# A two-layer hybrid block on one core: one shared pool of PSUM banks, new planner durations, two first projection blocks side by side, merged key-tile sums

## The chip, the core and the metric

The kernel runs on one core of a Trainium2 chip, as one program. The metric is the time of one execution on the device, in microseconds (us). The engines are TensorE (PE, matrix products; its weight loads are listed as PEld), VectorE (DVE), ScalarE (ACT), GpSimd (POOL) and SyncE (SP, which issues the DMAs here). TensorE writes to eight PSUM banks of 512 fp32 numbers per partition, and a matmul into a bank has to wait until what lay there before has been read.

## What is computed

Two layers over 528 positions (16 meta tokens and 512 inputs) with 1024 features, all in fp32. A layer is

```python
hn = rmsnorm(h, norm1_g[l])
sq, sk, sv, rq, rk, rv, rg, u = split(hn @ w_in[l])
sb_o = stick_breaking(rmsnorm(q), rmsnorm(k), v)      # 6 heads of 64
ro = retention(rotary(rmsnorm(q)), rotary(rmsnorm(k)), v)   # 6 heads of 64
ro = rmsnorm(ro) * silu(rg)
so = s5_mixer(u, ...)            # complex linear recurrence, 16 groups x 64 states
h = h + concat(sb_o, ro, so) @ w_out[l]
hn = rmsnorm(h, norm2_g[l])
h = h + (silu(hn @ w_gate[l]) * (hn @ w_up[l])) @ w_down[l]
```

In stick breaking a weight is exp(log_sigmoid(z) + between), where between is the sum of log_sigmoid(-z) over all later keys. The kernel gets these sums over keys as matmuls with matrices of ones.

## The kernel before

**Tiling.** Features lie on the 128 partitions, positions in the free dimension: a [128, 528] tile is one block of features, and a row of 528 takes two PSUM banks of 264 columns. Every large product is made of three fp32r products, of a high and a low part of the weights and of the activations (`mm3`, lines 347 to 356: for each block k of the contraction, wh*xh, wh*xl, wl*xh, each for two halves of the row). A weight block (`Unit`, line 273 on) is loaded by SP into one of two `wr` buffers, cast by ACT into its high part, and subtracted by DVE or POOL into its low part; four blocks are asked for ahead (`AHEAD`). A block of the input projection is 48 matmuls of 264 columns, and there are 23 of them in a layer.

**Side work.** Between two matmuls of a projection, `tick` (line 186) lets up to six waiting tasks go one step further. Tasks are Python generators: head norms, the lane of stick breaking (`sb_lane`, three pairs of heads one after the other), the lane of retention (`ret_lane`, three pairs) and the lane of the recurrence (`s5_lane`: `s5_mix` for two halves, then `s5_glu`). A task may go on when the time at which its last step should be done, by the planner, lies no later than `LEAD` after the planner's time on PE. The planner's durations stand in the three `Timed` wrappers (lines 125 to 127, a fixed part and a part for each element) and in `mm`. What is issued where follows from that; then a list scheduler orders each engine's queue, earlier-issued work first. On the chip each queue runs in that order. Nearly all instructions of DVE, ACT and POOL carry line 122 (the wrapper) and all matmuls line 134, so tiles are told apart by name.

**Banks.** The planner keeps count of banks: a task takes `banks(n)` out of `BANKS` = 2 (line 32) and gives them back after its result has been read; stick breaking takes its score banks out of a separate count `ZBANKS` = 4 (`take("scores", 2)`, line 872). Two of the eight banks are left for the projection that runs.

**The start.** `load_h(k)` (line 1037) loads the first weight block in four pieces right behind h[0] and ahead of h[1], and the second one whole behind h[4]. The first block's projection then runs alone, k by k, as `xh`, `xl` of h[k] come; the second and third follow. After the third (`HOLD` = 2) `nrm.finish` makes the norm's factors R. `first_params` is spawned ahead of all that: `s5_scalars` (line 452), a chain of some 95 small DVE instructions on [128, 16] tiles, and then `s5_params` (line 535), five tasks (`inputs` 0 and 1, `outputs`, `phasors` 0 and 1) on DVE and POOL, which `s5_lane` waits for (`par`). For the second layer `s5_params` runs during the first layer's MLP, on POOL alone.

**In `outputs`** (line 610), the imaginary half (`ri` = 1) is made on DVE by a `scalar_tensor_tensor` (-a - b) of two tiles `gx` that the engine of that half, POOL, has made.

**The sums of stick breaking** (`sb_group`, line 832). A group g is a list of key tiles (j, q0, q1, o0): key tile j, queries q0 to q1, at column o0 of a bank. `G_A` holds three key tiles for queries 0 to 272; `G_B2` three and `G_B1` two for queries 272 to 528. After two matmuls with the triangle `tri`, every key tile j of the group gets the sums of every later key tile i of the set: one pair of matmuls (high and low part) with `ones` for each pair (j, i). For `G_A` and `G_B2` these are 3 pairs with widths 144, 16 and 16; for `G_B1` they are 7, three of width 256, two of 144 and two of 16. Each set is made once for each of 6 heads in 2 layers.

## Time and profile before

| what | value |
|---|---|
| median of 3 runs (lowest to highest) | 1372.97 us (1372.7 to 1373.25) |
| profiled execution, its own time | 1372.14 us |
| span of that execution, first to last instruction | 1370.1 us |
| PE busy | 1335.6 us, 9188 matmuls |
| DVE, ACT, POOL busy | 791.4, 589.5, 464.9 us |
| mean granted TensorE clock | 0.994 |

The profiled execution is 0.83 us under the median, and 2.04 us of it lie outside the span. A row of a timeline gives the start and the length of an instruction, or of several in a row that are merged, their number (x), and in brackets how long the engine had been idle before it and what released it. A matmul's length includes its way through the array; what one more matmul costs in a row of them is the distance from start to start.

### The profile page before, as it was taken

Reading aid. Unit: us, or ns where it says so; the run is one execution under the profiler, and the core shown is the slowest. Engines: PE = TensorE matmul, PEld = TensorE weight load, DVE = VectorE, ACT = ScalarE, POOL = GpSimd, SP = SyncE. Lnnn points to the kernel's source line nnn. Section 1 sums busy time; section 2 is a strip of 40 time slices with the busy share of each in tenths; the row PEclk is TensorE's granted clock in tenths of the full one; section 3 lists DMA queues with packets and bytes.
Section 4 is the critical chain, followed back from the end, with each engine's and each line's share of the span. In section 5 each row is a group of like instructions: output and inputs, shape, how many; then the busy total and the mean of one; then the engine's idle time right before and its main releaser. Section 6 shows DMA issues by size and latency. Waiting matters only on the chain.

```text
span 1370.1 us, 22529 instructions
## 1 busy us (share of the span) xinstructions
PE 1335.6 (97%) x9188; PEld 1220.8 (89%) x9188; DVE 791.4 (58%) x1270; ACT 589.5 (43%) x936; POOL 464.9 (34%) x588
## 2 busy tenths in 40 slices
PE   6989999999899999999999999999999999999998
PEld 5988989989899999999999899998788888888886
DVE  8974657858456445533566874635485544554453
ACT  5447565446242223322355636664354422342231
POOL 5691545222799212200233451433222200220120
PEclk9999999999999999999999999999999999999999
DMA  4211222223221422232232221213232332333223
GB/s 157 70 62 47 84 66 87 78 69 98 95 79 48 123 78 93 93 93 93 78 93 93 71 94 47 92 43 102 62 123 93 92 95 90 99 102 93 92 81 104
DMA packets 38983, 118.26 MB, mean 86 GB/s; under 512 B 4960, under 2 KB 5472, under 8 KB 38880
## 3 DMA queue, kind: packets, MB, share of 16 engines
q1 hardware_dynamic: 38880, 116.82, 26.8%
q8 instruction: 72, 1.18, 0.4%
q14 instruction: 31, 0.25, 0.1%
HBM read 111.46 MB, written 2.10 MB: 83 GB/s over the span
## 4 chain that ended last, share of the span: by engine, by line
PE 82%; DVE 10%; POOL 3%; ACT 1%; issue 1%; DMA 1%; SPq 0%; DVEq 0%; ACTq 0%
PE pj L134 71%; PE z L134 5%; DVE ysm L122 2%; PE hps L134 1%; PE av L134 1%; PE ro L134 1%; DVE wl L122 1%; DVE s5w L122 1%; PE kps L134 1%; PE sc L134 1%; DVE gg L122 1%; DVE st L122 0%; DVE py L122 0%; POOL py L122 0%; DVE sp L122 0%
## 5 line engine op out<-in xcount | busy, mean ns | idle before, releaser
L134 PE MATMUL pj<-xh,wh 128*128 128x264 f32 (+1 forms) x1792 | 454.4, 311 | 16.8 <-ACT wh L122 5.1
L134 PE MATMUL pj<-xh,wl 128*128 128x264 f32 (+1 forms) x1792 | 453.3, 310 | 3.2 <-DVE wl L122 3.2
L134 PE MATMUL pj<-xl,wh 128*128 128x264 f32 (+1 forms) x1792 | 452.6, 310 | 2.6 <-DVE xl L122 2.6
L122 ACT CAST wh<-wr 128x1024 fp32r<-128x1024 f32 (+3 forms) x209 | 205.8, 987 | 418.8 <-PE pj L134 384.6
L134 PEld LDWEIGHTS pj<-xh,wh 128*128 128x128 f32 x1792 | 298.9, 190 | 36.0 <-issue 5.9
L134 PEld LDWEIGHTS pj<-xl,wh 128*128 128x128 f32 x1792 | 299.4, 190 | 20.5 <-DVE xl L122 3.3
L134 PEld LDWEIGHTS pj<-xh,wl 128*128 128x128 f32 x1792 | 298.9, 190 | 20.7 <-DVE wl L122 3.4
L122 DVE TENSOR_TENSOR wl<-wr,wh 128x1024 fp32r<-128x1024 f32 (+3 forms) x166 | 251.8, 1519 | 69.2 <-ACT wh L122 69.2
L134 PE MATMUL pj<-lo,wh 128*128 128x264 f32 (+1 forms) x720 | 193.4, 322 | 1.3 <-DVE lo L122 1.3
L134 PE MATMUL pj<-hi,wh 128*128 128x264 f32 (+1 forms) x720 | 193.2, 323 | 0.4 <-ACT hi L122 0.4
L134 PE MATMUL pj<-hi,wl 128*128 128x264 f32 (+1 forms) x720 | 193.1, 322 | 0.1
L122 POOL TENSOR_TENSOR up<-ga,up 128x528 f32<-128x528 f32 (+1 forms) x44 | 61.9, 1407 | 345.6 <-DVE up L122 345.5
L122 POOL TENSOR_TENSOR wl<-wr,wh 128x1024 fp32r<-128x1024 f32 (+2 forms) x43 | 96.2, 2237 | 159.4 <-ACT wh L122 153.6
L122 DVE TENSOR_TENSOR h<-h,pj 128x264 f32<-128x264 f32 (+1 forms) x144 | 69.1, 510 | 140.4 <-PE pj L134 140.0
L134 PEld LDWEIGHTS pj<-hi,wh 128*128 128x128 f32 x720 | 120.3, 189 | 11.9 <-ACT hi L122 0.7
L134 PEld LDWEIGHTS pj<-lo,wh 128*128 128x128 f32 x720 | 120.0, 188 | 12.1 <-DVE lo L122 1.5
L134 PEld LDWEIGHTS pj<-hi,wl 128*128 128x128 f32 x720 | 120.0, 189 | 11.1 <-DVE wl L122 0.5
L122 POOL TENSOR_TENSOR lo<-ga,hi 128x528 fp32r<-128x528 f32 (+1 forms) x44 | 58.5, 1330 | 158.0 <-ACT hi L122 157.9
L122 DVE TENSOR_TENSOR up<-pj,R 128x264 f32<-128x264 f32 (+1 forms) x66 | 32.1, 514 | 94.2 <-PE pj L134 94.2
L122 DVE TENSOR_TENSOR ga<-si,up 128x528 f32<-128x528 f32 (+1 forms) x44 | 31.7, 720 | 72.7 <-ACT si L122 57.2
L122 ACT ACTIVATE si<-si,bias 128x528 f32<-128x528 f32 (+1 forms) x44 | 32.2, 731 | 93.9 <-DVE si L122 93.9
L122 POOL TENSOR_TENSOR lo<-sp,hi 128x432 fp32r<-128x432 f32 (+2 forms) x36 | 44.4, 1245 | 73.3 <-ACT hi L122 71.7
(221 smaller groups left out, 1533.9 us busy)
## 6 DMA issues: line engine op xcount, KB each, us to landing
wr<-in_w_in_dram SPq DMA_DIRECT2D x45, 512.0 KB, 3.5
wr<-in_w_gate_dram SPq DMA_DIRECT2D x44, 512.0 KB, 3.5
wr<-in_w_up_dram SPq DMA_DIRECT2D x44, 512.0 KB, 3.5
wr<-in_w_down_dram SPq DMA_DIRECT2D x32, 512.0 KB, 3.6
wr<-in_w_out_dram SPq DMA_DIRECT2D x16, 384.0 KB, 3.3
wr<-in_w_down_dram SPq DMA_DIRECT2D x16, 384.0 KB, 3.1
rc<-in_rope_dram SPq DMA_DIRECT2D x12, 264.0 KB, 3.8
rs<-in_rope_dram SPq DMA_DIRECT2D x12, 264.0 KB, 4.0
```

Of the source, the lines that this page charges most:

```text
L122: return f(*a, **k)
L134: nc.tensor.matmul(out, lhsT=lhsT, rhs=rhs, start=start, stop=stop, skip_group_check=more)
```

## The change

Six edits: (1) all side work shares one count of six banks, of which stick breaking's scores may hold four at most; (2) the planner's durations are new, with a fixed part of 150 to 230 ns and other rates, by kind of instruction, and a double count for strided outputs; (3) the first two weight blocks are loaded and projected together, k by k (`two_proj`), with pieces of both between the h[k]; the squares of the norm are issued inside that loop, and `first_params` is spawned behind `nrm.finish`; (4) in `sb_group` the sums of one later key tile that go to two key tiles of the group are one matmul, whose moving operand is read twice and whose output has two pieces of the bank; (5) in `outputs` the half `ri` = 1 is an add on its own engine (POOL in both layers), with the sign moved into `bbd` and `xi`; (6) the task of `outputs` is planned 2 us later before the `kps` matmuls.

```diff
-BANKS = 2
+BANKS = 6
 ZBANKS = 4
...
-    V = Timed(nc.vector, "V", 70, 1.05)
-    SC = Timed(nc.scalar, "SC", 180, 0.7)
-    G = Timed(nc.gpsimd, "G", 110, 2.1)
+    V = Timed(nc.vector, "V", {"one": (150, 1.05), "two": (160, 1.2), "tensor_scalar": (150, 0.55),
+                               "tensor_tensor_scan": (180, 2.2)})
+    SC = Timed(nc.scalar, "SC", {"one": (230, 0.8), "two": (230, 0.8)})
+    G = Timed(nc.gpsimd, "G", {"one": (180, 2.1), "two": (180, 2.1), "memset": (100, 0.85)})
...
-                        if ri:
-                            V.scalar_tensor_tensor(out=o, in0=a, scalar=-1.0, in1=b, op0=ALU.mult, op1=ALU.subtract)
-                        else:
-                            sub(o, a, b)
+                        (add if ri else sub)(o, a, b)
...
-                    engines[ri].tensor_copy(
+                    engines[ri].tensor_scalar(
...
+            now[0][1] += 2000
...
-        behind = [(j, q0, q1, o0, i) for j, q0, q1, o0 in g for i in place if i > j]
...
+        behind = {}
+        for j, q0, q1, o0 in g:
+            for i, (g1, o1, p0) in place.items():
+                if i > j:
+                    a = max(q0, p0)
+                    behind.setdefault(i, (g1, o1 + a - p0, q1 - a, []))[3].append(o0 + a - q0)
...
+        for g1, o1, w, to in behind.values():
+            d, c = zp[:, to[0]:to[0] + w], slice(o1, o1 + w)
+            if len(to) == 2:
+                f = to[1] - to[0]
+                d = zp[:, to[0] + w - f:to[0] + w + f].rearrange("p (t c) -> p t c", t=2)[:, :, f - w:]
             for part in range(2):
-                mm(zp[:, o0 + a - q0:o0 + q1 - q0], lhsT=ones, rhs=hl[g1][part][:, o1 + a - p0:o1 + q1 - p0],
+                x = hl[g1][part][:, c]
+                mm(d, lhsT=ones, rhs=x[:, None, :].to_broadcast([P, 2, w]) if len(to) == 2 else x,
                    start=False, stop=True, more=True)
...
-        freed(1, "scores")
+        freed(1, "scores", "bank")
...
-                yield from take("scores", 2)
+                yield from take(2, "scores", "bank")
...
+    units += [Unit(*plan[0]), Unit(*plan[1])]
+    for k in range(KD):
         nc.sync.dma_start(out=h[k], in_=A["h0"][k])
...
+        q = []
+        if k < 4:
+            q = [(units[k % 2], k // 2, 4)]
+        elif k < 6:
+            q = [(units[k % 2], 1, 2)]
+        for u, i, pieces in q:
+            c = u.load(i, pieces)
+            nrm.parts(k)
+            for _ in u.split(c):
+                pass
+        if not q:
+            nrm.parts(k)
+        if k:
+            nrm.square(k - 1)
+    nrm.square(KD - 1)
...
-    spawn(first_params())
...
+        def two_proj():
+
+            ws = [weight(), weight()]
+            pss = [open_ps(T), open_ps(T)]
+            xh, xl = nrm.x
+            for k in range(KD):
+                for ps, w in zip(pss, ws):
+                    mm3(ps, tuple(t[:, k:k + 1, :] for t in w), (xh[k:k + 1], xl[k:k + 1]), first=k == 0, last=k == KD - 1)
+            return pss
...
             if i == HOLD[l]:
                 nrm.finish()
+                if l == 0:
+                    spawn(first_params())
```

## Rows read from the trace of the kernel before

**Rows 1.** The page, busy us (share of the span) xinstructions, PE.
```profile
PE 1335.6 (97%) x9188; PEld 1220.8 (89%) x9188; DVE 791.4 (58%) x1270; ACT 589.5 (43%) x936; POOL 464.9 (34%) x588
```
**Rows 2.** By stretch: length, busy PE PEld DVE ACT POOL, clock, DMA share, GB/s.
```profile
0.00:36.50 36.50, 23.50 (x148) 22.11 (x148) 30.51 (x97) 18.04 (x29) 21.85 (x45) 0.95 0.44 148
36.50:100.00 63.50, 58.15 (x437) 55.37 (x437) 53.49 (x139) 28.39 (x51) 50.52 (x117) 0.95 0.21 71
350.00:450.00 100.00, 94.75 (x764) 93.48 (x764) 54.52 (x68) 34.06 (x46) 94.35 (x208) 0.98 0.24 78
```
**Rows 3.** The same columns, in four us behind one of PE's longer waits.
```profile
30.00:34.00 4.00, 4.00 (x23) 4.00 (x22) 3.79 (x26) 1.32 (x2) 1.13 (x4) 0.57 0.64 255
```
**Rows 4.** Timeline of PE near 92 and 120 us: the sums of two groups.
```profile
92.17 0.23 PE L134 MATMUL z<-hi,ones 128*128 128x144 f32 x1
...
92.64 0.26 PE L134 MATMUL z<-lo,ones 128*128 128x16 f32 x1
92.75 0.49 PE L134 MATMUL pj<-xl,wh 128*128 128x264 f32 x2
...
119.73 0.39 PE L134 MATMUL z<-lo,tri 128*128 128x512 f32 x1
119.97 0.28 PE L134 MATMUL z<-hi,ones 128*128 128x256 f32 x1
...
120.21 0.23 PE L134 MATMUL z<-hi,ones 128*128 128x144 f32 x1
...
121.50 0.37 PE L134 MATMUL pj<-xh,wh 128*128 128x264 f32 x1
```
**Rows 5.** Timeline of PE in the first 36 us: start, length, idle before.
```profile
5.06 0.81 PE L134 MATMUL pj<-xh,wh 128*128 128x264 f32 x2 [5.06 <-ACT wh L122]
...
12.10 0.64 PE L134 MATMUL pj<-xh,wh 128*128 128x264 f32 x2
12.54 0.63 PE L134 MATMUL pj<-xl,wh 128*128 128x264 f32 x2
...
28.95 0.52 PE L134 MATMUL pj<-xh,wl 128*128 128x264 f32 x2 [3.19 <-DVE wl L122]
...
35.69 0.40 PE L134 MATMUL pj<-xh,wl 128*128 128x264 f32 x2
35.93 0.28 PE L134 MATMUL nps<-hi,meanw 128*128 128x264 f32 x1
```
**Rows 6.** Busy time by stretch of the instructions on tile s5w alone: DVE, ACT, POOL.
```profile
0.00:36.50 36.50, 18.70 (x65) 0.41 (x2) 0.00 (x0) 0.95 0.44 148
```
**Rows 7.** Timeline of DVE and POOL at 12.8 us: two instructions beside each other.
```profile
12.80 2.41 POOL L122 TENSOR_TENSOR wl<-wr,wh 128x1024 fp32r<-128x1024 f32 x1 [1.90 <-ACT wh L122]
12.93 2.38 DVE L122 TENSOR_SCALAR s5w<-s5w 128x16 f32<-128x16 f32 x2
```
**Rows 8.** Timeline of PE and DVE between 77 and 86 us.
```profile
77.44 0.39 PE L134 MATMUL pj<-xh,wh 128*128 128x264 f32 x1 [2.52 <-ACT we L122]
85.16 0.76 DVE L122 TENSOR_TENSOR u<-pj,R 128x264 f32<-128x264 f32 x2
```
**Rows 9.** Timeline of PE, DVE and POOL during the first layer's MLP.
```profile
371.61 0.56 PE L134 MATMUL pj<-xh,wh 128*128 128x264 f32 x1 [3.78 <-DVE ga L122]
368.07 2.94 DVE L122 SCALAR_TENSOR_TENSOR gg<-gx,gx 64x320 f32<-64x320 f32 x4 [3.96 <-POOL gx L122]
359.01 3.47 POOL L122 TENSOR_TENSOR gg<-gx,gx 64x320 f32<-64x320 f32 x4
413.51 0.41 PE L134 MATMUL kps<-gg,bbd 128*32 128x128 f32 x2 [1.47 <-POOL bbd L122]
```
**Rows 10.** Timeline of DVE and PE: the recurrence's lane in the first layer.
```profile
114.80 5.11 DVE L122 COPY uc<-u 32x132 f32<-32x132 f32 x8
155.17 1.06 PE L134 MATMUL es<-uc,we 128*128 128x132 f32 x8
281.96 0.51 PE L134 MATMUL pj<-lo,wh 128*128 128x264 f32 x2 [1.26 <-DVE lo L122]
```

More of the change, by code (lines that the diff above doesn't have):

```diff
@@ L107, in hybrid_kernel, with __init__ @@
     class Timed:
-        def __init__(self, eng, key, fixed, each):
-            self.eng, self.key, self.fixed, self.each = eng, key, fixed, each
+        def __init__(self, eng, key, kinds):
+            self.eng, self.key, self.kinds = eng, key, kinds
         def __getattr__(self, name):
@@ L117, in issue @@
                 o = k.get("out", a[0] if a else None)
-                n = 1
-                for d in o.shape[1:]:
-                    n *= d
-                spend(self.key, self.fixed + self.each * n)
+                n = math.prod(o.shape[1:]) * (2 if o.ap[-1][0] > 1 else 1)
+                two = [x for x in (k.get("in0"), k.get("in1")) if x is not None]
+                kind = name if name in self.kinds else "two" if len(two) == 2 and not any(
+                    x.space == PSUM for x in two) else "one"
+                fixed, each = self.kinds[kind]
+                spend(self.key, fixed + each * n)
                 return f(*a, **k)
             return issue
-    V = Timed(nc.vector, "V", 70, 1.05)
-    SC = Timed(nc.scalar, "SC", 180, 0.7)
-    G = Timed(nc.gpsimd, "G", 110, 2.1)
+    V = Timed(nc.vector, "V", {"one": (150, 1.05), "two": (160, 1.2), "tensor_scalar": (150, 0.55),
+                               "tensor_tensor_scan": (180, 2.2)})
+    SC = Timed(nc.scalar, "SC", {"one": (230, 0.8), "two": (230, 0.8)})
+    G = Timed(nc.gpsimd, "G", {"one": (180, 2.1), "two": (180, 2.1), "memset": (100, 0.85)})
     def mm(out, lhsT, rhs, start, stop, more=False):
-        n = out.shape[-1] / 2.4
-        t = 2 * max(107.0, 2 * n) if rhs.dtype == F32 else max(107.0, n) + 3
+        n = math.prod(out.shape[1:]) / 2.4
+        t = 2 * max(109.0, 2 * n + 3) if rhs.dtype == F32 else max(110.0, 1.055 * n + 5)
         spend("PE", t / 2 if 64 in (rhs.shape[0], out.shape[0]) else t)
@@ L172, in hybrid_kernel, with take, freed @@
     free = {"bank": BANKS, "scores": ZBANKS, "group": GROUPS}
-    def take(what, n):
-        if free[what] < n:
-            yield lambda: free[what] >= n
-        free[what] -= n
+    def take(n, *what):
+        if any(free[w] < n for w in what):
+            yield lambda: all(free[w] >= n for w in what)
+        for w in what:
+            free[w] -= n
     def banks(n):
-        yield from take("bank", n)
-    def freed(n, what="bank"):
-        free[what] += n
+        yield from take(n, "bank")
+    def freed(n, *what):
+        for w in what or ("bank",):
+            free[w] += n
     def tick(most=TICKS):
@@ L881, in sb_pair @@
         sets = ((G_A,), (G_B2, G_B1))
-        yield from take("group", 2)
+        yield from take(2, "group")
         started.append(weights(sets[0]))
@@ L887, in sb_pair @@
             if groups is sets[0]:
-                yield from take("group", 4)
+                yield from take(4, "group")
                 started.append(weights(sets[1]))
@@ L1034, in ret_pair @@
         res.append(o)
-    def load_h(k):
+    nrm = Norm(0, 48)
+    units += [Unit(*plan[0]), Unit(*plan[1])]
+    for k in range(KD):
         nc.sync.dma_start(out=h[k], in_=A["h0"][k])
@@ L1040, in load_h @@
             nc.sync.dma_start(out=cols, in_=A["cols"])
-            u = Unit(*plan[0])
-            u.parts = ()
-            for i in range(4):
-                for _ in u.split(u.load(i, 4)):
-                    pass
-            units.append(u)
-        elif k == 4:
-            u = Unit(*plan[1])
-            u.load()
-            u.parts = u.split()
-            units.append(u)
-            u.use()
-            splits[0] = 2
-    nrm = Norm(0, 48)
-    for k in range(KD):
-        load_h(k)
-        nrm.parts(k)
+        q = []
[13 more added lines that the diff above has]
+    nrm.square(KD - 1)
+    for u in units:
+        u.parts = ()
+    splits[0] = 2
     for i in (90, 96):
         G.tensor_scalar(out=cols[:, i:i + 2], in0=cols[:, i:i + 2], scalar1=0.125, scalar2=None, op0=ALU.mult)
-    for k in range(KD):
-        nrm.square(k)
     par = []
@@ L1075, in hybrid_kernel, with proj @@
         mix = [None] * 8
-        def proj(n, p):
-            w = weight()
+        def proj(w):
             ps = open_ps(T)
@@ L1129, in hybrid_kernel @@
         for i, (n, p) in enumerate(proj_order(l)):
-            held.append((n, p, proj(n, p)))
+            if l == 0 and i < 2:
+                if i == 0:
+                    first = two_proj()
+                held.append((n, p, first[i]))
+            else:
+                held.append((n, p, proj(weight())))
             if i == HOLD[l]:
                 nrm.finish()
+                if l == 0:
+                    spawn(first_params())
             if i >= HOLD[l]:
```

13 lines of the change are left out of this document (5 added, 8 removed).

## The prediction, made before the changed kernel was run

> **What bounds the kernel now.** I read the page first, then the busy time by stretch, then PE's timeline where it sits idle, then DVE and POOL at the same places. PE is busy 1335.6 of 1370.1 us [rows 1]: the reader is to see that only two things can be gained, PE's own work and its 34.5 us of idle time. The idle time is bunched: 36.50 - 23.50 = 13.0 us in the first 36.5, 63.50 - 58.15 = 5.35 us from there to 100, and 5.25 us between 350 and 450 [rows 2]; 10.9 us are scattered over the rest. A wait costs more than its length: after a wait of 3.19 us [rows 5] the granted clock was 0.57 over four us, the lower of its two levels (1.2 instead of 2.4 GHz) for 3.4 us of them, which is (1 - 0.57) x 4 = 1.7 us more [rows 3]. For the stretches, (1 - 0.95) x 63.5 = 3.2 us and (1 - 0.98) x 100 = 2.0 us [rows 2].
>
> **A, the merged sums.** Fewer matmuls in a stretch that PE bounds. A group of the kind of G_A or G_B2 issues six, from 92.17 to 92.75, 0.58 us; one of width 16 costs 0.11 [rows 4]. After it there are four: the pair of width 144, which stays, and one pair of width 32 for two pairs of width 16, at 0.11 each as before, so 0.22 less; as two neighbours of different width can share some of it, I take 0.19. G_B1 issues fourteen, 119.97 to 121.50, 1.53 us. After it eight: a pair of 256 at 0.24 (119.97 to 120.21), a pair of 512 at 2 x 0.24 (119.73 to 119.97), a pair of 288 at 0.27 (between those two), a pair of 32 at 0.22; 1.21 us, 0.32 less [rows 4]. 24 groups x 0.19 + 12 x 0.32 = 8.4 us, on the path, for 120 matmuls less. No row shows a moving operand that is read twice or an output in two pieces. From below: if a merged one costs as much as its two parts, 0. Worse: if each costs twice its width, 24 x 0.03 + 12 x 0.65 = 8 us are lost. I take -8.4, since width alone set the distance in every row here; ends +8 and -9.5.
>
> **B, the start.** A block is 48 matmuls at 0.12 (35.69 to 35.93 for two), three are 17.3 us; the third ends at 35.93 and the first matmul starts at 5.06 [rows 5], so 13.6 us are lost between them. One block alone offers six matmuls for each h[k], and h[1] stands in SP's queue behind four weight pieces; two blocks offer twelve, and h[1] stands behind one. SP issues 15 DMAs instead of 14, with the same bytes, so the last h[k] comes about when it did. Now the start: 5.06 (the first piece of weights still has to come) + 17.3 + the slow clock + a rest. At 12.10 two matmuls still take 0.44 instead of 0.24 [rows 5]; if the slow spacing again lasts to 13 us, 8 us hold 36 matmuls instead of 66, 3.6 us lost. DVE's s5w chain, 18.70 us busy in this stretch [rows 6], is out of it, so the wait for wl at 28.95, 3.19 us [rows 5], should go. The norm's squares move up in ACT's queue, between the high parts; ACT is busy 18.0 of 36.5 us [rows 2], so the cast of the third block behind them finds room. For the waits that stay (xl at DVE's pace, unit 1's low part behind POOL's constants) I put 2.5. Sum 28.5 us instead of 35.9: -7.4. Ends: no rest and a shorter slow stretch, -10; the third block's low part as late as now, with its clock, -2.5.
>
> **C, 36 to 100 us.** Waits and clock cost 5.35 + 3.2 = 8.5 us here [rows 2]. At 77.44 PE waits for a bank; the evacuation of block u, done before by DVE's queue order, comes at 85.16, behind a run of phasor instructions [rows 8]. The larger planned durations space those tasks, so evacuations fall between them. Against it: the s5w chain now comes behind the third block. DVE's 53.5 us [rows 2] + 18.7 [rows 6] - 2.9 (the subtractions that go to POOL, by the same work in [rows 9]) = 69.3 us, in the 71.5 us from 28.5 to 100. The three evacuations issued ahead of the chain free six banks, so PE has three blocks (17 us) before it misses the next evacuation; behind the chain wait the head norms' products and the low part of every third weight block. That is nearly full, so I take half the gain, -4; ends -8.5 and +8 (the second rival).
>
> A row speaks against moving the subtractions to POOL: a POOL subtraction ran from 12.80 for 2.41 us, and two DVE instructions of 16 columns beside it took 2.38 us together and ended with it [rows 7]. The Trainium skill (SBUF — State Buffer, section "SBUF: two separate sides") has it that the two engines share a pair of ports as an exclusive lock, held for the whole instruction, so that the loser stands still; the trace agrees. By that rule the four adds, 3.47 / 4 = 0.87 us each [rows 9], could stop DVE for up to 3.5 us in this stretch, C would be -0.5 and the time 3.5 us longer.
>
> **D, the MLP of the first layer.** PE waits 3.78 us at 371.61 for DVE to read ga; DVE had stood idle for 3.96 us at the head of its queue with the four subtractions gg, which wait for POOL's gx, and then worked on them for 2.94 us, with ga behind them [rows 9]. The change takes these four off DVE. Next late there: POOL's product up, on which DVE's later ga waits. POOL is busy 94.35 of 100 us [rows 2] and gets four more instructions, some 3.5 us [rows 9]. The wait of 1.47 us for bbd [rows 9] is what the 2 us of edit 6 are put against. The two are all 5.25 us of idle, with the clock 7.25 us; I take -6. Ends -7.25 and -2 (a POOL that is late by 3.5 us puts PE into a new wait).
>
> **E, the rest.** The shared banks remove no PE work. 10.9 us of idle are scattered outside B, C and D; some of it, as the last transfer of the output, nothing here touches, and 1.26 us are the wait for the recurrence's result at 281.96 [rows 10]. Two banks for all of head norms, retention and recurrence hold lanes back: uc is done at 114.80 + 5.11 = 119.9 and its first product es comes at 155.17, 35 us later [rows 10]. With six that should shrink. But stick breaking, which had four banks for itself, now competes; and PE comes about 20 us sooner to the output projection that needs the lanes. I take 0, ends -4 and +10. The signs moved in bbd and xi are the same instructions on the same engines: 0, bounded by tenths.
>
> **The sum.** -8.4 - 7.4 - 4 - 6 + 0 = -25.8 against the profiled execution's 1372.14 us: 1346.3. The median of the runs is 0.83 us above that execution: 1347.2.
>
> **Rivals.** (1) All waits in reach go: -9.5 - 10 - 8.5 - 7.25 - 4 = -39, 1334. For it: each has a cause that an edit names. Against: orders made anew make waits of their own. (2) DVE becomes the bound between 28 and 100: its idle time there is dependency and can't be used, so 18.7 - 2.9 = 15.8 us more work lengthen the stretch by 15.8 less the 7.4 of the earlier start: C is +8, 1359. For it: the 69.3 of 71.5 us. Against: part of the 18.70 are instructions held up by POOL [rows 7]. (3) The merged matmuls don't pay: A is 0 to +8, 1356 to 1364. (4) Slower: the recurrence is late. Its scalars now start behind nrm.finish, at some 30 us instead of 5, and the load of braw goes behind more weight loads in SP's queue with them; if the chain to uc keeps its length, uc starts at 114.8 + 25 = 140, and with a lane as long as now (114.8 to 281.96, 167 us [rows 10]) its result comes at 307. PE would be there at 281.96 - 7.4 - 4 - half of A = 266. It would wait up to 41 us, 1347 + 41 = 1388. It decides from 29 us on; below that the gain is larger than the wait. Against it: the 35 us between uc and es are a wait for banks that the change widens, and most of those 41 us are in them. (5) No change within what can be told: the new order gives back what the rest brings.
>
> **How the numbers follow.** Forecast, near 1347: 0.62. Rival 1: 0.08; rival 2: 0.12; rival 3: 0.07; rival 4: 0.08; rival 5: 0.03. The range for 8 in 10 runs from rival 1's 1334 to rival 3's 1364: it holds the forecast's, rival 2's and rival 3's 0.81, and leaves half of rival 1 below and 4 and 5 above. Faster by over 0.2% (2.7 us, about what a measurement of this kernel can tell from no change): 0.62 + 0.08 + 0.12 + 0.07 = 0.89; within it 0.03; slower 0.08.
>
> **What would show it.** A: 120 matmuls less, the sums of a G_B1 group within 1.2 us. B: nps at 27 to 30 us, no wait for wl ahead of it. C: no PE wait over one us and no half-clock stretch between 36 and 100; if rival 2 holds, waits for DVE's evacuations or wl there. D: no wait near 370 for ga, gg's four adds on POOL. E: es within some us of uc; PE waiting for lo of the recurrence at the output projection would be rival 4. Wrong would be the forecast, in its sum even if not in its parts, if PE's idle time stayed above 25 us.

## The result: slower by 1.2 per cent

| what | before | after |
|---|---|---|
| median (lowest to highest) of 4 runs each, same chip | 1373.1 us (1372.7 to 1373.25) | 1388.48 us (1387.08 to 1391.19) |
| ratio, 95% interval | | 1.0117 (1.0105 to 1.0129) |
| span of the profiled execution | 1370.1 us | 1389.5 us |
| mean granted clock | 0.994 | 0.978 |

The forecast was 1347; the time lies above its whole range, at the time of the fourth rival. The profiled execution of the changed kernel took 1391.19 us, 2.7 above its median.

First the page's line of busy times, of the changed kernel; it answers to [rows 1].

```profile
PE 1340.9 (97%) x9068; PEld 1222.3 (88%) x9068; DVE 784.7 (56%) x1261; ACT 588.1 (42%) x937; POOL 470.9 (34%) x598
```

The 120 matmuls are gone, and PE is nevertheless busy for 5.3 us longer and idle for 48.5 us instead of 34.5. Where, the busy time by stretch tells (length, busy PE, PEld, DVE, ACT, POOL, clock, DMA share, GB/s). The first two stretches are those of [rows 2]; then the rest of the in-projection; from the first matmul of the output projection's part (0,1,2) to the first of part (6,7); and six blocks of the first MLP, from the start of its fifth to the start of its eleventh. First the changed kernel:

```profile
0.00:36.50 36.50, 28.17 (x196) 27.32 (x196) 31.18 (x95) 19.61 (x33) 21.57 (x47) 0.95 0.49 162
36.50:100.00 63.50, 57.65 (x414) 53.55 (x413) 50.87 (x134) 33.10 (x62) 47.27 (x104) 0.92 0.19 63
100.00:253.30 153.30, 145.50 (x1096) 133.30 (x1094) 91.65 (x167) 78.49 (x153) 67.74 (x63) 0.96 0.23 73
253.30:304.40 51.10, 41.19 (x311) 37.89 (x309) 37.46 (x76) 20.93 (x41) 12.53 (x12) 0.85 0.12 37
360.20:409.70 49.50, 40.24 (x306) 39.63 (x305) 19.43 (x24) 15.90 (x23) 43.58 (x70) 0.86 0.21 70
```

The last three stretches of the same work in the kernel before:

```profile
100.00:252.40 152.40, 151.51 (x1204) 139.64 (x1202) 94.55 (x184) 85.28 (x164) 62.63 (x48) 1.00 0.23 73
252.40:280.20 27.80, 27.05 (x230) 25.52 (x226) 21.72 (x44) 18.22 (x33) 10.54 (x10) 1.00 0.21 58
344.40:386.10 41.70, 37.92 (x302) 37.74 (x301) 21.05 (x25) 13.49 (x18) 35.41 (x39) 0.96 0.24 83
```

The reader is to see the row of 253.3 to 304.4. Both kernels begin the output projection at the same moment, 252.4 and 253.3 us. The changed one then needs 51.1 us instead of 27.8: PE idles for 9.9 us of them (0.75 before), its clock is 0.85 (1.00 before), and it works off 311 matmuls instead of 230. 144 of either number are part (0,1,2); the rest, 167 and 86, is side work that the planner had left for this place (a row counts every matmul that overlaps its stretch; by their starts it is 165 and 81, as in the table below).

PE's timeline there, in the changed kernel, shows its waits: for retention's third pair (`kt`, `sc`, `hsq`) and for the recurrence's result (`hi`), which [rows 10] shows before. Below them stand two rows of ACT.

```profile
284.79 2.08 PE L138 MATMUL kv<-rv,kt 128*128 128x128 f32 x8 [5.26 <-ACT kt L125]
...
287.28 3.09 PE L138 MATMUL sc<-rm,rm 64*128 64x128 f32 x16 [0.25 <-DVE sc L125]
...
298.33 1.16 PE L138 MATMUL hps<-hsq,blk 128*128 128x264 f32 x4 [0.86 <-ACT hsq L125]
...
304.41 2.13 PE L138 MATMUL pj<-hi,wh 128*128 128x264 f32 x8 [3.46 <-ACT hi L125]
306.33 0.65 PE L138 MATMUL pj<-lo,wh 128*128 128x264 f32 x2
```
```profile
283.62 0.64 ACT L125 ACTIVATE y<-ysm 128x528 f32<-128x528 f32 x1 [3.80 <-DVE ysm L125]
284.17 0.57 ACT L125 COPY kt<-rtp 128x512 f32<-128x512 f32 x1
```

The longest wait, 5.26 us, is put down to retention's `kt`. But `kt` stands in ACT's queue right behind a step of the recurrence, `y`, for whose input ACT had waited 3.80 us; PE had made the input of `kt` by 279.5. So one lane holds up the other, by way of ACT's queue.

Adding up the two traces: PE's idle time +14.1 us (34.48 to 48.54); half of its busy time at the lower level (1.2 instead of 2.4 GHz, by the trace's record of the granted clock) +13.9 us (8.4 to 22.4); what is left, PE's work at the full level, -8.65 us (1327.2 to 1318.55). Together +19.4 us, the difference of the spans. Such a sum is good for some us only: PE's work at the full level differs between orders of the same matmuls as well (1318.55, 1312.5 and 1320.65 us in **after**, **j_after** and **j_after2** below).

### The profile page after: what moved, and what is told of

Same layout as the page of the kernel before. It is cut to its first block, busy times and chain, and to the rows that moved or that the text cites. A ratio compares the mean times of both kernels' runs of the same rounds, so it can differ in the third digit from the quotient of the medians.

```text
span 1389.5 us, 22290 instructions
## 1 busy us (share of the span) xinstructions
PE 1340.9 (97%) x9068; PEld 1222.3 (88%) x9068; DVE 784.7 (56%) x1261; ACT 588.1 (42%) x937; POOL 470.9 (34%) x598
## 4 chain that ended last, share of the span: by engine, by line
PE 82%; DVE 8%; POOL 5%; ACT 2%; issue 1%; DMA 1%; SPq 0%; DVEq 0%; ACTq 0%; POOLq 0%
PE pj L138 70%; PE z L138 4%; PE hps L138 2%; PE av L138 1%; PE ro L138 1%; DVE ysm L125 1%; DVE s5w L125 1%; POOL py L125 1%; POOL st L125 1%; DVE wl L125 1%; PE yps L138 1%; PE sc L138 1%; POOL gg L125 1%; POOL ws L125 1%; PE kps L138 1%
## 5 line engine op out<-in xcount | busy, mean ns | idle before, releaser
L125 DVE TENSOR_TENSOR wl<-wr,wh 128x1024 fp32r<-128x1024 f32 (+3 forms) x165 | 245.6, 1489 | 77.6 <-ACT wh L125 77.5
L125 POOL TENSOR_TENSOR wl<-wr,wh 128x1024 fp32r<-128x1024 f32 (+3 forms) x45 | 96.7, 2150 | 156.6 <-ACT wh L125 122.4
L138 PEld LDWEIGHTS pj<-hi,wl 128*128 128x128 f32 x720 | 120.7, 190 | 10.9 <-DVE wl L125 0.5
L138 PEld LDWEIGHTS pj<-lo,wh 128*128 128x128 f32 x720 | 120.9, 190 | 10.3
```

The costliest lines, as they stand in the source:

```text
L125: return f(*a, **k)
L138: nc.tensor.matmul(out, lhsT=lhsT, rhs=rhs, start=start, stop=stop, skip_group_check=more)
```

## The experiments

The kernels stand in the order of the questions. The ratio is to the kernel before on the same chip, with its 95% interval. "First layer" is the time from the start of the span to the last matmul of the first layer's down projection, "rest" the span less that; "side" is the number of matmuls between the first one of part (0,1,2) and the first one of part (6,7), less the matmuls of the parts between (144; 240 in x_parts); "idle" is PE's idle time there. HOP is a time in ns that the planner adds behind each planned step, 200 where nothing is said. "Early" and "late scalars" name the place in the program where `first_params` is spawned; where the chain then ran is told at u_late.

| kernel | median us | ratio | first layer | rest | side | idle |
|---|---|---|---|---|---|---|
| before | 1373.0 | | 719.0 | 651.1 | 81 | 0.75 |
| j_before (HOP 220) | 1382.94 | 1.0073 (1.0057 to 1.0088) | 729.2 | 653.3 | 134 | 8.9 |
| j_before2 (HOP 180) | 1376.12 | 1.0024 (1.0015 to 1.0034) | 718.4 | 656.1 | 85 | 3.8 |
| d_sums | 1381.63 | 1.0062 (1.0047 to 1.0077) | 730.0 | 650.2 | 105 | 10.9 |
| d_start | 1386.62 | 1.0103 (1.0086 to 1.0120) | 731.9 | 652.5 | 178 | 15.6 |
| c_ss | 1379.5 | 1.0044 (1.0028 to 1.0061) | 727.0 | 650.8 | 105 | 9.5 |
| u_dur | 1376.53 | 1.0033 (1.0020 to 1.0046) | 720.5 | 654.3 | 129 | 7.1 |
| c_de | 1368.0 | 0.9965 (0.9952 to 0.9978) | 710.9 | 654.5 | 69 | 3.4 |
| best1 | 1361.37 | 0.9916 (0.9902 to 0.9931) | 711.9 | 647.7 | 69 | 3.4 |
| jb_220 | 1355.77 | 0.9876 (0.9860 to 0.9893) | 709.3 | 644.6 | 93 | 3.1 |
| **after** | 1388.48 | 1.0117 (1.0105 to 1.0129) | 741.4 | 648.1 | 165 | 9.9 |
| j_after (HOP 220) | 1376.86 | 1.0032 (1.0020 to 1.0044) | 732.3 | 642.9 | 177 | 15.7 |
| j_after2 (HOP 180) | 1376.66 | 1.0025 (1.0015 to 1.0036) | 725.4 | 651.2 | 186 | 9.9 |
| u_late | 1375.38 | 1.0018 (1.0008 to 1.0027) | 725.0 | 648.1 | 169 | 10.3 |
| jl_220 | 1382.86 | 1.0069 (1.0054 to 1.0084) | 739.4 | 642.9 | 169 | 13.4 |
| jl_180 | 1384.83 | 1.0086 (1.0071 to 1.0101) | 732.2 | 650.9 | 177 | 9.6 |
| u_bank | 1384.54 | 1.0088 (1.0072 to 1.0103) | 736.4 | 647.2 | 154 | 15.2 |
| u_out | 1376.6 | 1.0022 (1.0010 to 1.0033) | 726.7 | 648.8 | 169 | 12.4 |
| x_prio | 1383.8 | 1.0078 (1.0060 to 1.0095) | 733.2 | 647.7 | 165 | 15.3 |
| x_parts | 1388.52 | 1.0113 (1.0098 to 1.0128) | 739.9 | 647.6 | 165 | 8.2 |

### One edit undone, or one alone

**u_dur**: the changed kernel with the old planner durations.

```diff
-    SC = Timed(nc.scalar, "SC", {"one": (230, 0.8), "two": (230, 0.8)})
+    SC = Timed(nc.scalar, "SC", 180, 0.7)
...
-        t = 2 * max(109.0, 2 * n + 3) if rhs.dtype == F32 else max(110.0, 1.055 * n + 5)
+        t = 2 * max(107.0, 2 * n) if rhs.dtype == F32 else max(107.0, n) + 3
```

> The changed kernel with the planner's old durations (V 70 + 1.05 n, SC 180 + 0.7 n, G 110 + 2.1 n, and the old matmul times); all other edits kept. In the changed kernel PE comes to the second part of the first layer's output projection 24 us later than before (304.4 instead of 280.2 us), because the recurrence is late. Theory durations: the larger planned times put each step of the recurrence's lane behind more of PE's work; then this kernel loses that wait and most of the 8 us in the first MLP, and comes to about 1356 us. Theory banks: the lanes compete for six banks in a bad order; then this kernel stays at 1380 to 1390. Theory late scalars: the recurrence's parameters start too late; then also 1380 to 1390.

Measured 1376.53, between the two expectations: the durations' undoing gives back 12 us; the first layer 21 us, while the rest gets 6 us longer.

**u_bank**: the changed kernel with two banks for side work and four score banks of their own.

```diff
-BANKS = 6
+BANKS = 2
-                yield from take(2, "scores", "bank")
+                yield from take(2, "scores")
```

> The changed kernel with the banks counted as before (two for side work, four for scores apart); all other edits kept. Theory banks: about 1362 us, the 24 us of the output projection gone. Theory durations and theory late scalars: no better than the changed kernel, 1385 to 1400, since the wait for banks between uc and es comes back on top.

Measured 1384.54, 4 us given back; 154 side matmuls are still left and PE idles longer among them, 15.2 us. The shared banks alone don't make the loss.

**d_sums**: the kernel before with the merged sums (edit 4) alone, as in the diff ahead of the prediction.

> The kernel before with the merged sums alone. By the prediction's term A: 8.4 us less, 1364.7 us. If a matmul that reads its moving operand twice costs as much as two: 1373. If the lanes and not PE set the time at the output projections, the saved PE time comes back as waits there: 1369 to 1373.

Measured 1381.63. A kernel that differs by 120 matmuls taken out of PE's queue, and by the order that follows from it, is 8.5 us slower. Its trace has PE's idle time at 46.0 us instead of 34.5, 10.9 of them in the drained stretch: the saved work came back as waits, and more than it. (Why 8.5 us are not yet a price of the edit, j_before shows.)

**d_start**: the kernel before with edit 3 alone, the late spawn of `first_params` among it.

> The kernel before with edit 3 alone: the first two blocks side by side, the squares between, the scalars of the recurrence behind the third block. By term B: 7.4 us less, 1365.7 us. Theory late scalars: PE waits for the recurrence at the first output projection, 1373 + 10 to 20 us = 1383 to 1393.

Measured 1386.62, though its third block ended at 29.75 us instead of 35.9; 178 side matmuls are left, and 15.6 us idle.

**u_late**: the changed kernel with the scalars early.

```diff
+    spawn(first_params())
     for l in range(LAYERS):
...
-                if l == 0:
-                    spawn(first_params())
```

> The changed kernel with the recurrence's scalars spawned ahead of the first block again, as before the change; all else as changed. Theory 'late scalars' (the move of first_params puts the recurrence's lane late, and TensorE waits for it): the first product kps comes at 95 to 97 us instead of 108, the recurrence's second yps at about 258 to 262 instead of 270 to 278, the idle and half-clock time of TensorE ahead of part (6,7) falls from 15.5 us to under 4, and the median from 1388.5 to about 1374 to 1377. Theory 'no slack' (the lanes of the first layer are chains that last as long as TensorE's work there; what is taken from TensorE's work comes back as a wait at the output projection, and any new issue order shifts which lane it is): kps comes earlier too, but part (345) still starts at 304 us or later, since retention's third pair comes behind; median 1378 to 1388.

Measured 1375.38, 13 us given back, as the fourth rival would have it. But the trace isn't that rival's: the stretch ahead of part (6,7) still holds 169 side matmuls and 10.3 us of idle time, the most of it put down to retention:

```profile
274.72 2.08 PE L138 MATMUL kv<-rv,kt 128*128 128x128 f32 x8 [8.77 <-ACT kt L125]
```

Nor were the scalars late in the changed kernel. On DVE their chain starts at 5.29 us and ends at 38.85 there, at 5.32 and 38.69 in u_late, and at 5.26 and 36.53 before; the busy time of `s5w` (DVE, ACT, POOL) in the changed kernel, to be held against [rows 6], is

```profile
0.00:36.50 36.50, 15.42 (x63) 0.41 (x2) 0.00 (x0) 0.95 0.49 162
```

The spawn came later in the program, but the chain stood as early in DVE's queue, in all twenty kernels here. So u_late tests an order of issue and nothing else.

**u_out**: the changed kernel with edits 5 and 6 undone (the four adds `gg` back on DVE as subtractions, no added 2 us).

> The changed kernel with the edit in outputs undone (the four adds gg back on VectorE as subtractions, no added 2 us); all else as changed. Theory 'POOL ahead of ws': the four adds of 4.46 us stood on POOL ahead of the memsets and sums ws that TensorE's transposes wait for; with them gone the waits of 8.20 and 1.06 us for ws near 397 shrink to under 1 us, the wait of about 3.8 us for ga comes back near 370, and the first layer's MLP from its fourth to its tenth block takes 42 instead of 49.5 us: median about 1382 to 1384. Theory 'durations': the early place of the transposes in TensorE's queue comes from the new durations alone, since with the old durations the same adds cost nothing there: the wait for ws stays over 4 us and the median over 1386. The adds of the first layer are also moved back, which changes its issue order by an amount that neither theory gives.

Measured 1376.6, 12 us given back, but only 4.9 us of it in the MLP (the six blocks 44.6 us instead of 49.5; the expectation counts blocks from 0), where the edit was aimed. There the wait for `ga` is back and that for `ws` is 2.09 us instead of 9.26:

```profile
377.37 0.56 PE L138 MATMUL pj<-xh,wh 128*128 128x264 f32 x1 [3.76 <-DVE ga L125]
```

**c_de**: the changed kernel with old durations and the early spawn, u_dur and u_late in one.

> The changed kernel with two edits undone: the old planner durations, and the scalars spawned ahead of the first block. Shared banks, merged sums, two first blocks side by side and the edit in outputs stay. Undoing the durations alone gave 1376.5. Theory 'late scalars': a further 10 us go, 1362 to 1368, with no wait over 1 us ahead of part (6,7). Theory 'no slack': the recurrence's lane comes earlier but retention's third pair still ends near 294 to 300 us, part (345) starts at 300 us or later, and the median is 1371 to 1378.

Measured 1368.0, faster than before, with 69 side matmuls left and 3.4 us of idle time ahead of part (6,7). It is the upper end of what the one theory gave, and below what the other allowed; the scalars' chain itself ran no earlier (5.24 to 38.31 us).

### Is it the edits, or the order that they happen to make?

Every undo that was tried gave back 4 to 13 us (the merged sums and the side-by-side start were not undone by themselves); for the durations, the spawn and the outputs it was 12, 13 and 12, which can't all be separate shares of 15.4. So a kernel with no edit at all was tried: **j_before** and **j_after** move one constant of the planner by a tenth, in the kernel before and in the changed one.

```diff
-HOP = 200
+HOP = 220
```

> The kernel before with one constant of the planner moved by a tenth: HOP, the time added behind each planned step, 220 instead of 200 ns. Nothing of what is computed changes, only the order of issue. Theory 'order' (each undo of an edit gave back 4 to 13 us because any change of the planner's input reshuffles the first layer's lanes; the order of before is one of the good ones): 5 to 15 us slower than before, 1378 to 1388, nearly all of it between 36 and 340 us. Theory 'edits' (the loss belongs to the edits themselves): within 3 us of before, 1370 to 1376.

> The changed kernel with the same constant moved by a tenth, HOP 220 instead of 200 ns. Theory 'order': the time moves by 4 us or more in either direction from 1388.5. Theory 'edits': it stays within 3 us, 1385.5 to 1391.5, and the scalars' and the durations' parts of the loss, 13 and 12 us, are what they seem.

Measured 1382.94, 10 us slower than before, and 1376.86, 12 us faster than after. Neither changes what is computed, or by which engine; only the order of issue differs. A single order can't tell an edit's own effect of under some 10 us from this. HOP isn't a mere shuffle, though: 220 makes every planned step longer, as edit 2 does, and j_before has 134 side matmuls where before has 81. So two more values each, **j_after2** and **j_before2** with HOP 180, and the same with early scalars, **jl_180** and **jl_220**.

> The changed kernel with HOP 180 instead of 200 ns, order of issue alone. HOP 200 gave 1388.5 and HOP 220 gave 1376.9. Theory 'order' (1388.5 is one draw of a spread of some 12 us): anywhere from 1372 to 1390. Theory 'late scalars in every order': all three lie above the same three with the scalars early, by about 13 us.

> The kernel before with HOP 180 instead of 200 ns, order of issue alone (200: 1373, 220: 1382.9). Theory 'order': 1373 to 1388; if it is above 1378, the order of before is the best of three and a mean of some 1380 is what the changed kernel's mean of 1380.7 has to be set against.

> The changed kernel with the scalars spawned ahead of the first block, HOP 180. At HOP 200 it ran 1375.4. Theory 'late scalars in every order': 1362 to 1378 and some 10 us under the changed kernel at HOP 180. Theory 'order': no fixed distance to it, above or below.

> The changed kernel with the scalars spawned ahead of the first block, HOP 220; the changed kernel at HOP 220 ran 1376.9. Theory 'late scalars in every order': 1362 to 1368. Theory 'order': 1370 to 1385, so the mean of three values of HOP with early scalars lies within 5 us of the mean with late ones.

The changed kernel at HOP 180, 200, 220: 1376.66, 1388.48, 1376.86, mean 1380.7. With early scalars: 1384.83, 1375.38, 1382.86, mean 1381.0. The 13 us of u_late were its draw: with the new durations the place of the spawn costs nothing that shows over three orders. The kernel before: 1376.12, 1373.0, 1382.94, mean 1377.4, of which the one that was changed is the best.

In all nine kernels with new durations in the first layer and the parts in their old order, 154 to 186 side matmuls are left for the drained stretch; with old durations 69 to 134, but for the 178 of d_start. The first layer's MLP doesn't hang on the draw: its six blocks take 48.7 to 49.9 us in the nine kernels with new durations and the moved adds (x_parts among them), and 41.6 to 42.6 in the ten with old durations.

**c_ss**: the kernel before with merged sums and the side-by-side start, early spawn; old durations, old banks, old outputs.

> The kernel before with two edits alone: merged sums, and the two first blocks side by side with the scalars spawned ahead of them as before. Old durations, two banks and own score banks, outputs as before. Theory 'late scalars': without the late start the two gains stand, 8 and 6 us: 1358 to 1362. Theory 'order' or 'no slack': TensorE's idle time between the in-projection and part (345) rises as in the run with the sums alone, and the median is 1368 to 1380.

Measured 1379.5: neither gain reaches the end here either. 9.5 us of idle time lie in the drained stretch, and another wait ahead of it, for the evacuation of `u` behind the recurrence's parameters on DVE:

```profile
80.56 0.59 PE L134 MATMUL pj<-xh,wh 128*128 128x264 f32 x1 [10.47 <-DVE u L122]
```

### Are the lanes late by their place, or by their length?

**x_prio**: the changed kernel, whose planner looks at the lanes of the recurrence and of retention first (`t[5]` is 0 for these two and 1 for all else).

```diff
-            for t in list(tasks):
+            for t in sorted(tasks, key=lambda t: t[5]):
```

> The changed kernel with one rule more in the planner: among the tasks that may go on, the recurrence's lane and retention's lane are looked at first, so they take banks and their place in the queues ahead of stick breaking and head norms. Theory 'place in the queues' (the two lanes end late since their steps are issued behind other side work): retention's second pair is issued before block 22, the idle and half-clock time ahead of part (6,7) falls from 15.5 us to under 8, median 1370 to 1381. Theory 'chain' (the lanes last as long as they last, whatever stands ahead): within 4 us of 1388.5.

Measured 1383.8, between the two expectations, with 165 side matmuls left and 15.3 us idle. So a lower rank among the waiting tasks isn't what makes the lanes late; the rule by which their steps are due stayed as it was.

**x_parts**: the changed kernel with another order of the output projection's parts.

```diff
-OUT_PARTS = (((0, 1, 2), (6, 7), (3, 4, 5)), ((6, 7), (0, 1, 2), (3, 4, 5)))
+OUT_PARTS = (((0, 1, 2), (3, 4), (6, 7), (5,)), ((6, 7), (0, 1, 2), (3, 4, 5)))
```

> The changed kernel with one order changed: the first layer's output projection takes the parts (0,1,2), (3,4), (6,7), (5) instead of (0,1,2), (6,7), (3,4,5): the same matmuls, with retention's first two pairs ahead of the recurrence and its third behind it. Theory 'no slack': when TensorE sits idle between 272 and 304 us, the results 3 and 4 are there; their 96 matmuls, 11.6 us, fill that time, the idle and half-clock time between the first and the third part falls from 15.5 us to 3 to 7, the parts end at about 326 instead of 336 and the median is 1377 to 1381. Theory 'late scalars' says the same here only if the recurrence's lane is all that is late: then part (6,7) starts without a wait. If TensorE waits as long as now, because the side work in its queue stands ahead of the new part, the median stays at 1386 to 1390 and the in-order queue itself is the cause.

Measured 1388.52, as the changed kernel; of the first theory's 7 to 11 us nothing came. Up to part (3,4) PE now doesn't wait at all (busy 25.10 of 25.1 us). From there to the end of the projection it waits as before, 8.2 us, and the last time at the start of part (6,7), for the recurrence's result:

```profile
275.40:329.70 54.30, 46.08 (x335) 43.44 (x334) 37.51 (x89) 22.88 (x43) 9.44 (x9) 0.87 0.18 52
```
```profile
309.68 2.13 PE L138 MATMUL pj<-hi,wh 128*128 128x264 f32 x8 [3.10 <-ACT hi L125]
```

So 96 matmuls of PE's own work, put ahead of part (6,7), didn't cover the waits: the last of the 96 starts at 291.8 us, the side work of both lanes stands among and behind them in PE's queue, and part (6,7) starts at 309.7 instead of 304.4. That is nearest to the third outcome of the expectation.

### A version that beats both

Three pairs of kernels differ by the durations alone while the first layer is planned: after and u_dur, u_late and c_de, jl_220 and jb_220. With the old ones the first layer is 20.9, 14.1 and 30.1 us shorter, 7.1 to 7.6 of that in the six blocks of the MLP. Over all orders it takes 725.0 to 741.4 us in the ten kernels with new durations, and 709.3 to 720.5 in the four that have old ones and the other edits. For the rest the new durations are better (647.4 us as a mean of three orders, 653.5 before). **best1** takes c_de and changes the durations over at the second layer; **jb_220** is best1 with HOP 220.

```diff
+                if old[0]:
+                    fixed, each = OLD[self.key]
+                    n = math.prod(o.shape[1:])
...
     for l in range(LAYERS):
+        old[0] = l == 0
```

> The changed kernel with the scalars spawned ahead of the first block, the old durations while the first layer is planned and the new ones from the second layer's in-projection on. The first layer ended at 710.9 us with the old durations and early scalars; from there to the end the new durations took 648.1 us in two runs, the old ones 654.5. If the two layers are independent: span 1359, median 1361 to 1362. If the second layer's gain belongs to the planner's state carried over from the first: 1365 to 1369.

> The fastest version so far (1361.4: early scalars, old durations for the first layer, new ones for the second) with HOP 220 instead of 200 ns. Theory 'order': 8 to 20 us slower, 1369 to 1381, the loss between 36 and 330 us and the second layer within 2 us of 648. If the edits themselves made it fast: 1359 to 1364.

Measured 1361.37 and 1355.77, 11.5 and 17.4 us under before. The first layers agree within 2.6 us at the two values of HOP that were tried; jb_220 is faster than either expectation had it, 2.6 us by the first layer and 3.1 by the rest. Its drained stretch, the part behind it and the MLP's (jb_220; columns as above):

```profile
249.00:280.20 31.20, 28.10 (x239) 26.93 (x238) 25.30 (x52) 18.95 (x36) 9.06 (x9) 1.00 0.16 48
280.20:309.40 29.20, 29.20 (x241) 29.17 (x240) 22.06 (x41) 15.58 (x25) 9.68 (x6) 1.00 0.30 96
334.40:376.80 42.40, 37.51 (x303) 36.67 (x301) 19.70 (x22) 14.28 (x18) 36.45 (x42) 0.95 0.25 88
```

Against the changed kernel's rows: 31.2 us instead of 51.1, clock 1.00 instead of 0.85. Where the recurrence stands, its products `yps` tell, from the first to the last start (line, operation, number: shortest, median and longest ns, first and last start, form): changed kernel, jb_220 and before.

```profile
L138 PE MATMUL yps<-uc,tz x16: 273/276/380, 194.3 to 277.8; 128*128 128x132 f32 x16
```
```profile
L146 PE MATMUL yps<-uc,tz x16: 275/276/380, 159.4 to 245.4; 128*128 128x132 f32 x16
```
```profile
L134 PE MATMUL yps<-uc,tz x16: 273/276/276, 181.4 to 246.0; 128*128 128x132 f32 x16
```

In the two faster kernels the last of them comes before the output projection begins (249.0 and 252.4 us), in the changed one 24.5 us behind (253.3).

## Why the prediction was wrong

The prediction named an idle time of PE above 25 us as what would show it wrong; it is 48.5. Term by term:

**A, the merged sums: right in itself.** A group of the kind of G_B1 takes 113.88 - 112.69 = 1.19 us, where 1.21 was forecast; 0.23 for 512 columns in two pieces, 0.13 to 0.14 for 288.

```profile
112.69 0.39 PE L138 MATMUL z<-hi,ones 128*128 128x512 f32 x1
112.92 0.40 PE L138 MATMUL z<-lo,ones 128*128 128x512 f32 x1
113.15 0.30 PE L138 MATMUL z<-hi,ones 128*128 128x288 f32 x1
...
113.88 0.40 PE L138 MATMUL z<-hi,tri 128*128 128x512 f32 x1
```

PE's work at the full level fell by 8.65 us for the -8.4 of the sum, and it fell in the other orders too (HOP 220: 1328.3 to 1312.5 us; HOP 180: 1327.8 to 1320.65). So rival 3 is out. The step that failed is "on the path". d_sums has 6.5 us less of that work and 11.5 us more idle time. In the second layer a gain hardly shows either: with merged sums and old durations the rest of the span is 650.2, 650.8, 654.3 and 654.5 us (d_sums, c_ss, u_dur, c_de), mean 652.5, against 653.5 over the three orders before, where half of A was 4.2. What goes below that, 642.9 to 651.2, has the new durations.

**B, the start: near in size, not by the cause that was named.** `nps` comes at 29.54 for 35.93 [rows 5], 6.4 us sooner where 7.4 were forecast. The wait for the third block's low part is gone; one for the second half of the first block's came, at 16.93. DVE's chain, which the sum had "out of it", is still there: 15.42 us for 18.70 [rows 6], and two of its instructions stand right ahead of that low part. What the start gained, it gained beside the chain.

```profile
16.93 0.81 PE L138 MATMUL pj<-xh,wl 128*128 128x264 f32 x2 [2.46 <-DVE wl L125]
...
29.54 0.28 PE L138 MATMUL nps<-hi,meanw 128*128 128x264 f32 x1
```
```profile
13.82 1.34 DVE L125 TENSOR_TENSOR s5w<-s5w 128x16 f32<-128x16 f32 x2
15.08 1.79 DVE L125 TENSOR_TENSOR wl<-wr,wh 128x512 fp32r<-128x512 f32 x1
```

**C, 36 to 100 us: wrong sign.** Idle time and clock there cost 5.85 + 0.08 x 63.5 = 10.9 us, for 8.5 before and the 4.5 of the forecast. Rival 2 isn't it: its condition, the chain behind the third block, didn't come about, and DVE is busy 50.87 of 63.5 us, less than before [rows 2]. For the same reason the forecast's own "nearly full", for which it took half the gain, was without ground. And the wait of 2.52 us in [rows 8] was for ACT's `we`; `u` cost PE 0.83 us there (at 85.64), so spacing the phasors aimed at the smaller of the two. In the changed kernel the longest wait, 2.52 us again, is for `u`, behind a phasor run. DVE's timeline, and POOL's and PE's beside it, show more:

```profile
75.88 2.31 DVE L125 TENSOR_TENSOR st<-st 128x4 f32<-128x4 f32 x1
```
```profile
75.83 2.34 POOL L125 TENSOR_TENSOR wl<-wr,wh 128x1024 fp32r<-128x1024 f32 x1
```
```profile
78.48 0.42 DVE L125 TENSOR_TENSOR u<-pj,R 128x264 f32<-128x264 f32 x1
```
```profile
78.96 0.59 PE L138 MATMUL pj<-xh,wh 128*128 128x264 f32 x1 [2.52 <-DVE u L125]
```

An instruction of DVE on 4 columns, which takes 0.15 to 0.22 us in the rows around it (one more took 1.02 us, beside POOL's 1.10), lasted as long as POOL's on 1024 columns and ended with it; `u` came behind it, and PE's wait of 2.52 us has about its length. That is the Trainium skill's rule that was weighed in the prediction (SBUF — State Buffer, section "SBUF: two separate sides"): an exclusive lock on a shared pair of ports, for the whole instruction. The trace agrees; the wait came by a low part of the weights, though, not by the four adds that were moved to POOL. The kernel before has such a pair too (2.63 us on POOL at 79.26, 2.34 on DVE at 79.58, 4 columns), and PE had work then: the edits changed when the lock comes, not whether.

**D, the first layer's MLP: wrong sign.** The wait for `ga` at 371 [rows 9] is gone, as forecast. "A POOL that is late by 3.5 us puts PE into a new wait" was one end of the range. A new wait is what came, larger, but not by a later POOL. POOL's timeline and PE's:

```profile
384.49 4.46 POOL L125 TENSOR_TENSOR gg<-gx,gx 64x320 f32<-64x320 f32 x4
...
394.99 6.39 POOL L125 TENSOR_TENSOR ws<-btmp,btmp 64x256 f32<-64x256 f32 x8
```
```profile
397.71 1.97 PE L144 MATMUL wps<-ident,ws 128*128 128x128 f32 x8 [8.20 <-POOL ws L125]
400.74 1.12 PE L144 MATMUL wps<-ident,ws 128*128 128x128 f32 x4 [1.06 <-POOL ws L125]
```

The four adds stand on POOL ahead of `ws`, for which PE's transposes wait 9.26 us, and the granted clock over the six blocks is 0.86 instead of 0.96. They take 49.5 us instead of 41.7, +7.8 for a forecast of -6. With the old durations and the same adds they take 42.2 to 42.4 (u_dur, c_de, best1, jb_220), some 0.6 more than before, so there the edit changes one wait for another: 4.5 to 5.1 us for `ws` instead of 3.8 for `ga`. With the new durations and the adds undone (u_out) it is 44.6. In u_dur the wait is

```profile
382.87 1.97 PE L140 MATMUL wps<-ident,ws 128*128 128x128 f32 x8 [2.45 <-POOL ws L122]
```

POOL ends `ws` as late after the MLP's first matmul in either kernel, 65.3 us (336.1 to 401.4) and 65.8 (321.7 to 387.5). PE, however, comes to the transposes 53.4 us after it in the changed kernel (389.5) and 58.7 in u_dur (380.4). So it isn't a later POOL: the new durations put the transposes 5.3 us, nearly a block, earlier into PE's queue, ahead of what they wait for. Two steps are missing: what lies behind the moved work in its new engine's queue and who waits for that, and what edit 2 does to the place of the waiting matmuls.

**E, the rest: the term that decided.** It was put at 0, with ends -4 and +10. Measured between 100 us and part (6,7): idle time 7.8 + 9.9 us instead of 0.9 + 0.75, and by the clock 0.04 x 153.3 + 0.15 x 51.1 = 13.8 us instead of none, of which a part lies in that idle time. Two steps failed. One: edit 2 was costed only in C, as something that lets evacuations through. Longer planned durations also put every step of a lane of many steps later against PE's blocks, so the lanes reach the output projection with 165 matmuls to go instead of 81. The wait between uc and es did shrink, as forecast: es comes at 151.5 us for 155.2, though uc starts at 130.2 for 114.8. But from there to the last `yps` it is 126 us instead of 91. PE, with little else left, waits at one link of them after the other. That edit 2 is the cause, the three pairs of kernels show; that it works by the due times rather than by the rank among tasks is supported by x_prio, not proved by it, and which of the new durations does it stays open. Two: the sum took PE's work and waits as things that can be removed one by one. In the first layer the lanes ended with PE, 1.26 us behind it [rows 10], so there was no slack into which a saving could go, unless the lanes come sooner as well; where they do (c_de, best1, jb_220), the first layer is 7 to 10 us shorter than before, near A's half of 4.2 and B's 6.4. A to D as measured (-8.65, -6.4, +2.4, +7.8) come to -4.9; for the spans to differ by +19.4, E must be some +24 us.

**Rival 4** gave 1388, the place of the wait and the point from which it decides, and it got 0.08. Its cause is not the one that was measured. Its first condition didn't hold: the scalars did not start at 30 us but where they did before, at 5.29 for 5.26, and their chain ended 2.3 us later. `kps` comes at 108 instead of 95, so the delay is behind the chain, in the parameters made from it; and where the spawn stands, over three orders, makes no difference with the new durations (1381.0 early, 1380.7 late). With the old durations the one pair there is (u_dur and c_de) has 9.5 us in the first layer between them; one draw each, so what the late spawn costs there stays open.

**The range** left out the size of what couldn't be priced: an order made anew. With one constant moved by a tenth the kernels moved by 10 and 12 us. Of the loss of 15.4 us, the means over three orders leave 3.3 (1380.7 against 1377.4); the remaining 12 are that before stood on its best draw of three and after on its worst. What holds in each of the three orders is smaller and of both signs (profiled executions): at the same HOP `nps` comes 4.7 to 8.5 us sooner, the six MLP blocks take 7.2 to 8.0 us longer and the rest of the span is 3.0 to 10.4 us shorter. The stretch from `nps` to the MLP's fifth block is 11.4 us longer on the mean, and there the draws differ most (1.8 to 22.2). Three draws don't make a distribution; that the sign of the whole holds over all orders isn't shown (at HOP 220 the changed kernel is the faster one).

## What to carry to other kernels

Before PE's work is counted as time, look where the side chains end: if they end with PE, a saving needs them to end sooner too, and here a planner told of longer durations moved them later. When an edit moves a task in the program, look in the trace whether its instructions moved: here the scalars didn't. Where a planner makes the order, move one of its constants by a tenth first; that spread, here 10 to 12 us, is what a single run of an edit has to beat, and several orders of either kernel are what to compare. Of work moved to an idle engine, look up what stands behind it in that engine's queue and who waits for that.

## What the hardware showed beyond that

A matmul whose moving operand is read twice and whose output lies in two pieces of a bank cost as much here as a plain one of as many columns: 0.23 us for 2 x 256, 0.24 for 512 [rows 4]. Waits that follow each other cost the clock as well: over the drained stretch and the six MLP blocks the granted clock was 0.85 and 0.86, which is 7.7 and 6.9 us beside 9.9 and 9.3 us of idle time (some of it the same time). The four adds `gg` took 4.46 us on POOL beside a DVE instruction that overlapped the second of them, and 3.47 without, both in the changed kernel.
